# Indexer scores without POOL, and a convolution's running sum in PSUM

## The chip, the cores and the metric

One core of a Trainium2 chip runs the whole program. The metric is device time in microseconds (us), the median over runs of the same kernel. A profile is one further execution, recorded by the hardware profiler. The engines are PE (TensorE, matmuls), DVE (VectorE), ACT (ScalarE), POOL (GpSimd) and SP (SyncE, which here issues transfers). Matmuls write to PSUM, which is used here as eight banks of 128 partitions by 512 fp32 numbers; DVE and ACT read and write both PSUM and SBUF, and POOL is used here on SBUF alone.

## The reference

One decoder layer on 512 tokens of width 1024, batch 1, everything in fp32. After an RMSNorm, one projection is split between a gated DeltaNet group (4 heads) and a sparse attention group; both are joined, and a cross attention and a SwiGLU feed-forward follow. Two places matter here. The first is the input of the DeltaNet heads: 12 blocks of 128 channels (q, k and v for 4 heads), each put through a causal convolution with four taps per channel and then silu. The second is the score of the indexer, which decides the 128 keys that each query keeps:

```python
dq, dk, dv, dz, db, da, cq, ckv, kix, wix = jnp.split(h @ w_in[l], offs, axis=-1)
qkv = jax.nn.silu(causal_depthwise_conv(jnp.concatenate([dq, dk, dv], axis=-1), conv_w[l]))
...
rel = jax.nn.relu(jnp.einsum('bqhd,bsd->bqhs', qi, k_idx))       # 8 indexer heads
score = jnp.einsum('bqh,bqhs->bqs', wi, rel).astype(jnp.float32)
score = jnp.where(key_pos[None, None, :] <= tq[None, :, None], score, -jnp.inf)
_, idx = lax.top_k(score, k_sel)                                 # k_sel = 128
```

## The kernel before

Tokens run along the free dimension, channels along the partitions. fp32 matmuls are made from parts: every operand is split into a high and a low part, and `dense` (L149 to L151) issues three matmuls per 128 rows of the contraction, 24 for a projection of 128 channels. Weights come by DMA (`wraw`), ACT makes the high part `wh` (L141), and POOL or DVE subtracts it to give the low part `wl` (L142).

The order of the text is not the order on the chip. A scheduler reorders the instructions of each engine before the launch, within what data and buffers allow. The stages, as they are written: the input columns of the sparse group; transposes and norms (L328 to L331); the indexer's scores (L400 to L419, with the mask of future keys by POOL's `affine_select` in L421); four projections (k0, q0, k1, q1); gates and decays of the DeltaNet heads (L428 to L465, `Dm` and `row` among their names); top-k by 16 rounds of `max` (L489, eight values at a time) and `match_replace` (L490) for each of three query tiles, ended by L493; the other eight projections; `vt` (L540), a product for the attention; preparation of the triangular systems (L637 to L671); inverses of their diagonal blocks on DVE (L678 to L718), which go through DRAM (`x_d`) and come back as `X`; two further levels of the inverse on PE (L726 on), the recurrence, the attention, and the dense layers, from about 275 us to the end.

`project` (L352 to L381) makes one block of channels: dense into a PSUM bank `o`; L367 (DVE) multiplies by the row of norms into `cp`; L369 and L377 (ACT) make two taps from shifted copies, `a` and `b`; L378 and L379 (DVE) add the other two taps to them; L380 (POOL) adds `a` and `b`, and L381 (ACT) applies silu. For two of the v blocks (m 9 and 11) a third tap is ACT's (L373), added by POOL (L374), and DVE has only L375.

The scores: for each of 8 heads and each of 3 query tiles (256, 384 and 512 keys) two matmuls fill a bank `oo[s]`. For heads other than 2 and 6 DVE takes relu and the weight in one operation (L414), from PSUM into one of four buffers of `rlb`, and POOL adds it to the score (L416); the first head writes the score itself. For heads 2 and 6 ACT takes relu into `rlb` (L418), and DVE multiplies by the weight and adds (L419).

PSUM banks in this phase have the tags g (3 banks), lg (2), tp (2) and o (1). `ps(tag)` gives a bank: "pj", used by the first four projections, means tp; "mm", used by the other eight, means lg and tp in turn; "at", used by the scores and most else, goes through g, g, lg, g, o, lg.

Of the kernel before, what the change touches and what calls it, by code (L numbers as in the profile page):

```python
# [10 lines left out]
FT = mybir.dt.float32  # L11
FR = mybir.dt.float32r
AF = mybir.ActivationFunctionType
OP = mybir.AluOpType
AX = mybir.AxisListType

T = 512
# [64 lines left out]
def hybrid_block(ctx, tc, I, out):  # L82
    nc = tc.nc
    pe, act, dve, pool, sp = nc.tensor, nc.scalar, nc.vector, nc.gpsimd, nc.sync
# [19 lines left out]
    def pool_of(name, side=None):  # L104
        return tc.alloc_tile_pool(name=name, bufs=1, reuse_waits="tile", side=side) if side else \
            tc.alloc_tile_pool(name=name, bufs=1, reuse_waits="tile")
# [15 lines left out]
    def ps(tag="at"):  # L122
        n_ps[0] += 1
        if tag not in banks:
            turn[tag] = turn.get(tag, -1) + 1
            tag = alias[tag][turn[tag] % len(alias[tag])]
        return banks["pool"].tile([128, 512], FT, name=f"ps{n_ps[0]}", tag=tag, bufs=banks[tag])
# [40 lines left out]
    def weights(src, k0, kt, c0, cols, sub=None):  # L168
        return weights_split(*weights_raw(src, k0, kt, c0, cols), sub)

    def dense(h, l, XH, XL, n=T, o=None, order=None):
        o = ps("mm")[:, :n] if o is None else o
        order = order or range(len(XH))
        for k in order:
            mm3(o, h[:, k, :], l[:, k, :], XH[k], XL[k], k == order[0], k == order[-1])
        return o
# [42 lines left out]
    def par(name, k=0):  # L219
        return prT[:, PAR[name] + k:PAR[name] + k + 1]  # L220
# [75 lines left out]
    gp = pool_of("gp", "right")  # L296
# [1 line left out]

    wq = gp.tile([128, 2, 2, 512], FR, name="wq", tag="NT")
    wu = gp.tile([128, 2, 2, 512], FR, name="wu", tag="OGl")  # L300
    rlb = gp.tile([128, 4, 512], FT, name="rlb", tag="A")
    for w_, name in ((wq, "w_qidx"), (wu, "w_uq")):
        raw, _ = weights_raw(I[name][0], 0, 2, 0, 512)
        split(w_[:, 0], w_[:, 1], raw)
# [5 lines left out]
    for t in range(NT):  # L310
# [13 lines left out]
        for d in range(2):  # L324
            dve.tensor_scalar(kx[:, t * 128 + 64 * d:t * 128 + 64 * d + 64], kix_, st[:, 0:1], rs[:, 0:1],
                              op0=OP.subtract, op1=OP.mult)
        dve.scalar_tensor_tensor(ckv_, ckv_, rs[:, 2:3], gkv_b, op0=OP.mult, op1=OP.mult)
        for d in range(2):  # L328
# [4 lines left out]
                          None, op0=OP.mult)  # L333
# [18 lines left out]
    def project(kind, h, bank="mm", sub=pool):  # L352
        def c(shape=(128, T)):
            n_t[0] += 1
            return cvp.tile(list(shape), FT, name=f"cp{n_t[0]}", tag="cp", bufs=6)

        m = {"q": h, "k": 4 + h, "v": 8 + h}[kind]
        wh, wl = weights(w_in, 0, 8, m * 128, 128, sub)
        o = dense(wh, wl, XH, XL, o=ps(bank))
        if kind == "k" and QK[h] is None:  # L360
            QK[h] = gdn.tile([128, 2, T], FT, name=f"QK{h}", tag=f"QK{h}")
        if kind == "v":
            vtok[h] = gdn.tile([128, NT, 128], FT, name=f"vtok{h}", tag=f"vtok{h}")
        dst = vtok[h].rearrange("p c d -> p (c d)") if kind == "v" else QK[h][:, 0 if kind == "k" else 1, :]
        cp = c((128, T + 4))
        pool.memset(cp[:, 0:3], 0.0)
        dve.tensor_tensor(cp[:, 3:T + 3], o, Rrow, op=OP.mult)  # L367
        a, b = c(), c()
        act.activation(a, cp[:, 0:T], AF.Identity, scale=par("conv_w", m))  # L369
        if m in (9, 11):  # L370
            d_ = c()
            act.activation(b, cp[:, 1:T + 1], AF.Identity, scale=par("conv_w", 12 + m))
            act.activation(d_, cp[:, 2:T + 2], AF.Identity, scale=par("conv_w", 24 + m))  # L373
            pool.tensor_tensor(b, b, d_, op=OP.add)  # L374
            dve.scalar_tensor_tensor(a, cp[:, 3:T + 3], par("conv_w", 36 + m), a, op0=OP.mult, op1=OP.add)  # L375
        else:
            act.activation(b, cp[:, 1:T + 1], AF.Identity, scale=par("conv_w", 12 + m))  # L377
            dve.scalar_tensor_tensor(a, cp[:, 2:T + 2], par("conv_w", 24 + m), a, op0=OP.mult, op1=OP.add)  # L378
            dve.scalar_tensor_tensor(b, cp[:, 3:T + 3], par("conv_w", 36 + m), b, op0=OP.mult, op1=OP.add)  # L379
        pool.tensor_tensor(a, a, b, op=OP.add)  # L380
        act.activation(dst, a, AF.Silu)  # L381


    masks = dsa.tile([128, 1152], FT, name="masks")
# [1 line left out]
    score = {t: masks[:, SEG[t][0]:SEG[t][0] + SEG[t][1]] for t in SEG}  # L386
# [13 lines left out]
    for pr_ in range(4):  # L400
        st = qst[pr_]
        for t in (1, 2, 3):
            n = SEG[t][1]
            tt = slice(t * 128, (t + 1) * 128)
            oo = [ps()[:, :n] for _ in range(2)]
            for s in range(2):
                pe.matmul(oo[s], st[s][:, tt], kidl[:, :n], start=True, stop=False)
                pe.matmul(oo[s], st[s][:, tt], kidh[:, :n], start=False, stop=True)
            for s in range(2):
                hd = 2 * pr_ + s  # L410
                rl = rlb[:, (pr_ * 6 + t * 2 + s) % 4, :n]
                w_ = widx[:, 8 * t + hd:8 * t + hd + 1]
                if hd not in (2, 6):
                    dve.tensor_scalar(rl if hd else score[t], oo[s], 0.0, w_, op0=OP.max, op1=OP.mult)  # L414
                    if hd:
                        pool.tensor_tensor(score[t], score[t], rl, op=OP.add)  # L416
                    continue
                act.activation(rl, oo[s], AF.Relu)  # L418
                dve.scalar_tensor_tensor(score[t], rl, w_, score[t], op0=OP.mult, op1=OP.add)  # L419
    for t in (1, 2, 3):  # L420
        pool.affine_select(score[t][:, t * 128:], score[t][:, t * 128:], pattern=[[-1, 128]], compare_op=OP.is_ge,  # L421
                           fill=FUT, base=0, channel_multiplier=1)
# [1 line left out]
    for kind, h in (("k", 0), ("q", 0), ("k", 1), ("q", 1)):  # L424
        project(kind, h, bank="pj", sub=dve)
# [410 lines left out]
    for i, (kind, h) in enumerate([(k, h) for h in (2, 3) for k in "kq"] + [("v", h) for h in range(4)]):  # L836
        steps(gt, 1 if i % 2 else 2)
        project(kind, h)
# [6 lines left out]
    A = gp.tile([128, 4, NT, 128], FT, name="A", tag="A")  # L845
# [287 lines left out]
```

## Time and profile before

| what | us |
|---|---|
| median of 3 runs | 857.08 (856.7 to 859.29) |
| profiled execution | 855.63 |
| its span (first to last instruction) | 853.8 |
| PE busy in the span | 824.2 |

In the rows below, engines and operations are named as above; "x4" behind an operation means that the row groups four instructions, and a row of a timeline gives start, duration, and in brackets how long the engine was idle before it and what it waited for. Durations of neighbouring instructions of an engine can overlap a little.

### The profile page before, as it was taken

To read this page: it belongs to the slowest core of one execution; us is meant where nothing else is said; L and a number is where in the kernel's file an instruction comes from. 1 tells how busy PE (TensorE), PEld (TensorE's weight loads), DVE (VectorE), ACT (ScalarE), POOL (GpSimd) and SP (SyncE) were. 2 spreads that over 40 slices of the span, in tenths; PEclk is the share of its full clock that TensorE was granted. 3 is DMA by queue.
4 is the path that set the end of the run, shared out by engine and by line. 5 is a ranking of instruction groups with operands and counts; after the bars stand their busy time and mean duration, and the time that the engine had idled before them with its cause. 6 is when DMAs were issued, how large, how long until landed. Compare 5 with 4: busy or idle time off the path is not lost.

```text
span 853.8 us, 11022 instructions
## 1 busy us (share of the span) xinstructions
PE 824.2 (97%) x4122; PEld 679.5 (80%) x4122; DVE 489.6 (57%) x817; ACT 366.3 (43%) x721; POOL 211.4 (25%) x217
## 2 busy tenths in 40 slices
PE   9998999779998999999999999999999999999996
PEld 8876787578766889888877888888888888888885
DVE  7787999967555545464555445543355443245542
ACT  6675666417656544354444442221133331223332
POOL 5549577853211231000003221110011110001122
PEclk9999999889999999999999999999999999999999
DMA  8530322146525234343313533333323333332302
GB/s 288 149 102 26 125 74 72 35 95 165 131 57 198 68 93 137 99 137 107 96 55 106 166 99 99 91 92 111 91 83 99 99 98 99 99 90 83 99 25 98
DMA packets 134940, 88.30 MB, mean 103 GB/s; under 512 B 10304, under 2 KB 122344, under 8 KB 134888
## 3 DMA queue, kind: packets, MB, share of 16 engines
q1 hardware_dynamic: 131848, 85.87, 34.5%
q10 hardware_dynamic: 3040, 1.75, 0.7%
q8 instruction: 32, 0.52, 0.3%
q14 instruction: 20, 0.16, 0.1%
HBM read 76.84 MB, written 4.99 MB: 96 GB/s over the span
## 4 chain that ended last, share of the span: by engine, by line
PE 79%; DVE 12%; POOL 2%; ACT 2%; issue 2%; DMA 2%; SPq 0%; POOLq 0%; DVEq 0%; ACTq 0%
PE ps L149 21%; PE ps L150 21%; PE ps L151 21%; DVE masks L490 3%; DVE m L489 2%; DVE cp L378 1%; PE ps L607 1%; PE ps L1078 1%; PE ps L1077 1%; PE ps L1076 1%; PE ps L291 1%; PE ps L952 1%; PE ps L954 1%; PE ps L953 1%; POOL masks L416 1%
## 5 line engine op out<-in xcount | busy, mean ns | idle before, releaser
L141 ACT ACTIVATE wh<-wraw 128x1024 fp32r<-128x1024 f32 x120 | 127.7, 1065 | 314.7 <-PE ps L150 169.4
L151 PE MATMUL ps<-XH,wl 128*128 128x512 f32 x512 | 201.0, 393 | 0.0
L149 PE MATMUL ps<-XH,wh 128*128 128x512 f32 x512 | 200.6, 392 | 0.2 <-ACT wh L141 0.2
L150 PE MATMUL ps<-XL,wh 128*128 128x512 f32 x512 | 199.9, 390 | 0.0
L142 DVE TENSOR_TENSOR wl<-wraw,wh 128x1024 fp32r<-128x1024 f32 x108 | 154.3, 1430 | 67.9 <-ACT wh L141 67.6
L149 PEld LDWEIGHTS ps<-XH,wh 128*128 128x128 f32 x512 | 96.2, 188 | 20.7 <-issue 0.6
L151 PEld LDWEIGHTS ps<-XH,wl 128*128 128x128 f32 x512 | 96.1, 188 | 19.7 <-POOL wl L142 0.3
L150 PEld LDWEIGHTS ps<-XL,wh 128*128 128x128 f32 x512 | 96.2, 188 | 19.5
L1047 POOL TENSOR_TENSOR t2k<-t2k,t2k 128x512 f32<-128x512 f32 x22 | 29.4, 1336 | 291.0 <-DVE t2k L1046 283.9
L258 POOL TENSOR_TENSOR acc<-acc,t2k 128x512 f32<-128x512 f32 x21 | 37.4, 1779 | 182.2 <-ACT t2k L257 181.8
L1046 DVE TENSOR_TENSOR t2k<-ps,row 128x512 f32<-128x512 f32 x22 | 15.2, 691 | 67.9 <-PE ps L151 67.9
L151 PE MATMUL ps<-HH,wl 128*128 128x512 f32 x128 | 50.0, 393 | 0.0
L149 PE MATMUL ps<-HH,wh 128*128 128x512 f32 x128 | 49.9, 390 | 0.0
L150 PE MATMUL ps<-HL,wh 128*128 128x512 f32 x128 | 49.6, 390 | 0.0
L1058 DVE TENSOR_TENSOR XR<-ps,XR 128x512 f32<-128x512 f32 x16 | 11.1, 692 | 51.9 <-PE ps L151 51.9
L1044 DVE TENSOR_TENSOR t2k<-ps,row 128x512 f32<-128x512 f32 x22 | 15.2, 691 | 36.0 <-PE ps L151 36.0
L142 POOL TENSOR_TENSOR wl<-wraw,wh 128x1024 fp32r<-128x1024 f32 x12 | 29.5, 2464 | 18.4 <-ACT wh L141 18.4
L888 DVE TENSOR_TENSOR XR<-ps,XR 128x512 f32<-128x512 f32 x16 | 11.0, 691 | 34.0 <-PE ps L151 34.0
L489 DVE MAX8 m<-masks 128x8 f32<-128x512 f32 (+2 forms) x48 | 26.7, 556 | 4.4 <-POOL masks L421 3.6
L150 PEld LDWEIGHTS ps<-HL,wh 128*128 128x128 f32 x128 | 24.0, 188 | 5.1
L151 PEld LDWEIGHTS ps<-HH,wl 128*128 128x128 f32 x128 | 24.0, 188 | 4.9
L149 PEld LDWEIGHTS ps<-HH,wh 128*128 128x128 f32 x128 | 24.0, 188 | 4.9
(398 smaller groups left out, 1659.3 us busy)
## 6 DMA issues: line engine op xcount, KB each, us to landing
wraw<-in_w_gate SPq DMA_DIRECT2D x22, 512.0 KB, 3.6
wraw<-in_w_up SPq DMA_DIRECT2D x22, 512.0 KB, 3.7
wraw<-in_w_down SPq DMA_DIRECT2D x20, 512.0 KB, 3.8
wraw<-in_w_in SPq DMA_DIRECT2D x16, 512.0 KB, 3.7
wraw<-in_w_xkv SPq DMA_DIRECT2D x16, 512.0 KB, 3.8
wraw<-in_w_out SPq DMA_DIRECT2D x8, 512.0 KB, 4.0
wraw<-in_w_xq SPq DMA_DIRECT2D x8, 512.0 KB, 3.7
wraw<-in_w_xo SPq DMA_DIRECT2D x8, 512.0 KB, 3.8
```

Of the source, the lines that this page charges most:

```text
L141: act.activation(h, src, AF.Copy)
L142: (sub or dve).tensor_tensor(l, src, f32(h), op=OP.subtract)
L149: pe.matmul(o, lh, rh, start=start, stop=False)
L150: pe.matmul(o, lh, rl, start=False, stop=False)
L151: pe.matmul(o, ll, rh, start=False, stop=stop)
L258: pool.tensor_tensor(self.acc, self.acc, s_, op=OP.add)
L489: dve.max(m8, score[t])
L490: dve.match_replace(score[t], m8, score[t], MARK)
L1044: dve.tensor_tensor(s1, og_, Rrow2, op=OP.mult)
L1046: dve.tensor_tensor(s2, ou_, Rrow2, op=OP.mult)
L1047: pool.tensor_tensor(s1, s1, s2, op=OP.mult)
L1058: dve.tensor_tensor(XR[m], o, XR[m], op=OP.add)
```

## The change

Two edits. In the scores, the buffers `rlb` go; for heads 1 to 7 ACT takes relu in place, in the PSUM bank, and DVE multiplies that by the head's weight and adds it to the score. Head 0 stays as it was. POOL has no part in it any more. In `project`, the running sum `a` lies in a PSUM bank of the same kind as `o`: ACT writes the first tap there, DVE adds the second-last tap there, and the last tap is added by DVE into a new SBUF buffer `e_`, to which POOL adds `b`. For m 9 and 11, DVE reads `a` from PSUM too. Since both `o` and `a` now come from the tags "mm" or "pj", a projection takes two banks in turn instead of one. Lines of the new kernel are lower by 1 from L302 on and by 3 from L420 on.

```diff
-    rlb = gp.tile([128, 4, 512], FT, name="rlb", tag="A")
...
         dve.tensor_tensor(cp[:, 3:T + 3], o, Rrow, op=OP.mult)
-        a, b = c(), c()
+
+        a, b = ps(bank), c()
         act.activation(a, cp[:, 0:T], AF.Identity, scale=par("conv_w", m))
         if m in (9, 11):
             d_ = c()
             act.activation(b, cp[:, 1:T + 1], AF.Identity, scale=par("conv_w", 12 + m))
             act.activation(d_, cp[:, 2:T + 2], AF.Identity, scale=par("conv_w", 24 + m))
             pool.tensor_tensor(b, b, d_, op=OP.add)
-            dve.scalar_tensor_tensor(a, cp[:, 3:T + 3], par("conv_w", 36 + m), a, op0=OP.mult, op1=OP.add)
         else:
             act.activation(b, cp[:, 1:T + 1], AF.Identity, scale=par("conv_w", 12 + m))
             dve.scalar_tensor_tensor(a, cp[:, 2:T + 2], par("conv_w", 24 + m), a, op0=OP.mult, op1=OP.add)
-            dve.scalar_tensor_tensor(b, cp[:, 3:T + 3], par("conv_w", 36 + m), b, op0=OP.mult, op1=OP.add)
-        pool.tensor_tensor(a, a, b, op=OP.add)
-        act.activation(dst, a, AF.Silu)
+        e_ = c()
+        dve.scalar_tensor_tensor(e_, cp[:, 3:T + 3], par("conv_w", 36 + m), a, op0=OP.mult, op1=OP.add)
+        pool.tensor_tensor(e_, e_, b, op=OP.add)
+        act.activation(dst, e_, AF.Silu)
...
-                rl = rlb[:, (pr_ * 6 + t * 2 + s) % 4, :n]
                 w_ = widx[:, 8 * t + hd:8 * t + hd + 1]
-                if hd not in (2, 6):
-                    dve.tensor_scalar(rl if hd else score[t], oo[s], 0.0, w_, op0=OP.max, op1=OP.mult)
-                    if hd:
-                        pool.tensor_tensor(score[t], score[t], rl, op=OP.add)
+                if hd == 0:
+                    dve.tensor_scalar(score[t], oo[s], 0.0, w_, op0=OP.max, op1=OP.mult)
                     continue
-                act.activation(rl, oo[s], AF.Relu)
-                dve.scalar_tensor_tensor(score[t], rl, w_, score[t], op0=OP.mult, op1=OP.add)
+                act.activation(oo[s], oo[s], AF.Relu)
+                dve.scalar_tensor_tensor(score[t], oo[s], w_, score[t], op0=OP.mult, op1=OP.add)
```

The scheduler also moves instructions. Three places follow, each as the rows of one engine in their order.

PE, the end of the first projection (`ps_655`) and the start of the second (`ps_697`) before, and the rows between the two after; the lines L328 to L331 are transposes of the input `U`:

```order
L151 MATMUL ps_655<-XH_91,wl_652 128x512
L331 MATMUL ps_347<-cst,U_148 128x128 [waits DVE_49,PE_49]
L149 MATMUL ps_697<-XH_84,wh_693 128x512 [waits Activation_49]
L150 MATMUL ps_697<-XL_92,wh_693 128x512
L151 MATMUL ps_697<-XH_84,wl_694 128x512
```

```order
L328 MATMUL ps_343<-cst,U_148 128x128 [waits Activation_49]
L328 MATMUL ps_344<-cst,U_148 128x128 [waits PE_49]
L329 MATMUL ps_345<-cst,t2k_347 128x128 [waits PE_49]
L328 MATMUL ps_343<-cst,U_149 128x128 [waits Activation_49]
L328 MATMUL ps_344<-cst,U_149 128x128
L328 MATMUL ps_343<-cst,U_150 128x128 [waits Activation_49]
L328 MATMUL ps_344<-cst,U_150 128x128
L329 MATMUL ps_345<-cst,t2k_347 128x128 [waits DVE_49]
L330 MATMUL ps_346<-cst,U_149 128x128 [waits DVE_49]
L329 MATMUL ps_345<-cst,t2k_347 128x128 [waits DVE_49]
L330 MATMUL ps_346<-cst,U_150 128x128 [waits DVE_49]
L149 MATMUL ps_697<-XH_84,wh_693 128x512 [waits DVE_49]
```

The second projection waits for DVE now, where it waited for ACT, and eleven transposes stand ahead of it.

DVE, the start of the scores, before and after (`masks` holds the scores, `sm_349` and `sm_348` the heads' weights, `prT` the taps, `cp_` and `ps_811` the convolution's buffers):

```order
L414 TENSOR_SCALAR masks<-ps_523,sm_349 128x256 [waits PE_49]
L414 TENSOR_SCALAR masks<-ps_532,sm_349 128x384 [waits PE_49]
L414 TENSOR_SCALAR rlb<-ps_524,sm_349 128x256 [waits PE_49]
L378 SCALAR_TENSOR_TENSOR cp_809<-cp_806,prT,cp_809 128x512 [waits Activation_49,Pool_49]
L414 TENSOR_SCALAR rlb<-ps_533,sm_349 128x384 [waits PE_49]
L414 TENSOR_SCALAR masks<-ps_541,sm_349 128x512 [waits PE_49]
L379 SCALAR_TENSOR_TENSOR cp_810<-cp_806,prT,cp_810 128x512 [waits Activation_49]
L414 TENSOR_SCALAR rlb<-ps_542,sm_349 128x512 [waits PE_49,Pool_49]
```

```order
L413 TENSOR_SCALAR masks<-ps_522,sm_348 128x256 [waits PE_49]
L413 TENSOR_SCALAR masks<-ps_531,sm_348 128x384 [waits PE_49]
L377 SCALAR_TENSOR_TENSOR ps_811<-cp_808,prT,ps_811 128x512 [waits Activation_49,Pool_49]
L413 TENSOR_SCALAR masks<-ps_540,sm_348 128x512 [waits PE_49]
L379 SCALAR_TENSOR_TENSOR cp_816<-cp_808,prT,ps_811 128x512 [waits DVE_49]
L416 SCALAR_TENSOR_TENSOR masks<-ps_523,sm_348,masks 128x256 [waits Activation_49]
L416 SCALAR_TENSOR_TENSOR masks<-ps_532,sm_348,masks 128x384 [waits Activation_49]
L416 SCALAR_TENSOR_TENSOR masks<-ps_541,sm_348,masks 128x512 [waits DVE_49,Activation_49]
```

The waits for POOL at the reuse of `rlb` are gone, and every multiply-add waits for ACT's relu.

DVE, the last rounds of top-k and the end of the diagonal blocks, before and after (L710 before and L707 after is the copy that is sent to DRAM):

```order
L489 MAX m_991<-masks 128x8 [waits DVE_49]
L710 COPY cv_1786<-cv_1762 128x256 [waits DVE_49]
L490 MATCH_REPLACE masks<-m_991,masks 128x512 [waits DVE_49]
L489 MAX m_991<-masks 128x8 [waits DVE_49]
L493 TENSOR_SCALAR masks<-masks 128x512
L490 MATCH_REPLACE masks<-m_991,masks 128x384 [waits DVE_49]
L489 MAX m_991<-masks 128x8 [waits DVE_49]
L493 TENSOR_SCALAR masks<-masks 128x384
L490 MATCH_REPLACE masks<-m_991,masks 128x256 [waits DVE_49]
L493 TENSOR_SCALAR masks<-masks 128x256 [waits DVE_49]
```

```order
L700 TENSOR_TENSOR cv_1776<-cv_1771,cv_1773 128x512 [waits DVE_49]
L702 TENSOR_REDUCE cv_1777<-cv_1776 128x64 [waits DVE_49]
L703 TENSOR_TENSOR cv_1776<-cv_1773,cv_1777 128x512 [waits DVE_49]
L705 TENSOR_REDUCE cv_1773<-cv_1776 128x8x8 [waits DVE_49]
L707 COPY cv_1797<-cv_1773 128x256 [waits DVE_49]
L725 TENSOR_TENSOR cv_1822<-ps_1817,cst 128x512 [waits PE_49]
```

Before, the last of the top-k instructions stood behind the copy; now the copy is the last of this stretch.

## Rows read from the trace of the kernel before

**Rows 1.** The page's first part: busy time, share of the span, instructions.

```profile
PE 824.2 (97%) x4122; PEld 679.5 (80%) x4122; DVE 489.6 (57%) x817; ACT 366.3 (43%) x721; POOL 211.4 (25%) x217
```

**Rows 2.** Busy time by stretch: stretch, length, engines (instructions), PE clock, DMA share, GB/s.

```profile
61.40:85.90 24.50, 22.25 (x104) 15.02 (x104) 19.19 (x32) 14.80 (x36) 22.42 (x22) 1.00 0.12 32
85.90:106.30 20.40, 19.28 (x88) 15.20 (x87) 19.48 (x54) 12.79 (x48) 11.10 (x16) 1.00 0.39 130
106.30:176.10 69.80, 64.47 (x285) 51.17 (x285) 68.85 (x151) 38.15 (x100) 50.71 (x44) 0.95 0.21 55
183.30:275.00 91.70, 84.44 (x658) 68.70 (x658) 56.67 (x157) 55.51 (x178) 27.57 (x41) 0.98 0.52 140
275.00:853.80 578.80, 571.13 (x2700) 476.95 (x2699) 272.35 (x326) 200.90 (x294) 67.89 (x54) 1.00 0.33 97
```

**Rows 3.** Timeline of DVE, 36 to 180 us: start, duration, what it does.

```profile
36.67 0.68 DVE L367 TENSOR_TENSOR cp<-ps,row 128x512 f32<-128x512 f32 x1
...
61.41 1.00 DVE L414 TENSOR_SCALAR masks<-ps,sm 128x256 f32<-128x256 f32 x2
...
85.89 0.69 DVE L489 MAX8 m<-masks 128x8 f32<-128x512 f32 x1 [3.58 <-POOL masks L421]
...
106.31 0.69 DVE L367 TENSOR_TENSOR cp<-ps,row 128x512 f32<-128x512 f32 x1 [0.24 <-PE ps L151]
...
116.44 2.92 DVE L378 SCALAR_TENSOR_TENSOR cp<-cp,prT,cp 128x512 f32<-128x512 f32 x1
...
175.73 0.39 DVE L710 COPY cv<-cv 128x256 f32<-128x256 f32 x1
...
179.38 0.29 DVE L493 TENSOR_SCALAR masks<-masks 128x256 f32<-128x256 f32 x1
```

**Rows 4.** Timeline of PE, 33 to 184 us.

```profile
33.82 0.48 PE L149 MATMUL ps<-XH,wh 128*128 128x512 f32 x1
...
100.44 0.58 PE L149 MATMUL ps<-XH,wh 128*128 128x512 f32 x1
...
106.12 0.39 PE L149 MATMUL ps<-XH,wh 128*128 128x512 f32 x1
...
183.28 5.99 PE L726 MATMUL ps<-X,NTt 128*128 128x128 f32 x32 [4.40 <-DMA X<-x_d]
```

**Rows 5.** POOL by shape, 61.4 to 86: instructions, busy us, mean ns, idle before.

```profile
L416 POOL TENSOR_TENSOR masks<-masks,rlb 128x512 f32<-128x512 f32 x5 | 6.6, 1314 | 0.0
L421 POOL TENSOR_SCALAR_AFFINE_SELECT masks<-masks 128x128 f32<-128x128 f32 x3 | 0.8, 287 | 0.1
```

**Rows 6.** DVE by shape, 61.4 to 85.9 us.

```profile
L414 DVE TENSOR_SCALAR rlb<-ps,sm 128x512 f32<-128x512 f32 x5 | 3.7, 745 | 1.1 <-POOL masks L416 1.0
L414 DVE TENSOR_SCALAR rlb<-ps,sm 128x384 f32<-128x384 f32 x5 | 3.0, 609 | 0.5 <-POOL masks L416 0.5
L414 DVE TENSOR_SCALAR rlb<-ps,sm 128x256 f32<-128x256 f32 x5 | 2.4, 478 | 0.1
L419 DVE SCALAR_TENSOR_TENSOR masks<-rlb,sm,masks 128x512 f32<-128x512 f32 x2 | 1.5, 739 | 0.0
```

**Rows 7.** Timeline of ACT, 77 to 100 us.

```profile
77.35 0.98 ACT L418 ACTIVATE rlb<-ps 128x512 f32<-128x512 f32 x2 [0.28 <-DVE masks L419]
...
87.94 1.22 ACT L141 ACTIVATE wh<-wraw 128x1024 fp32r<-128x1024 f32 x1
...
98.26 1.10 ACT L540 ACTIVATE vt<-ps 128x512 f32<-128x512 f32 x2
```

**Rows 8.** DVE by shape, 106.3 to 176.1 us.

```profile
L378 DVE SCALAR_TENSOR_TENSOR cp<-cp,prT,cp 128x512 f32<-128x512 f32 x6 | 10.5, 1752 | 0.0
L379 DVE SCALAR_TENSOR_TENSOR cp<-cp,prT,cp 128x512 f32<-128x512 f32 x6 | 4.8, 796 | 0.0
L375 DVE SCALAR_TENSOR_TENSOR cp<-cp,prT,cp 128x512 f32<-128x512 f32 x2 | 3.7, 1863 | 0.0
```

**Rows 9.** Timeline of POOL, at 116 us.

```profile
116.40 2.40 POOL L142 TENSOR_TENSOR wl<-wraw,wh 128x1024 fp32r<-128x1024 f32 x1
```

## The prediction

> **What bounds the kernel now.** I read the page's first part, then the busy times by stretch, then the timelines of the four engines at the places where the change acts. TensorE is busy for 824.2 us, 97% of the span [rows 1], so only what shortens its gaps or its slow stretches can move the end. The stretches show where those are [rows 2]: from 275 us on, PE is busy for 571.13 of 578.8 us with dense matmuls, and nothing in the change touches that. The change acts between 61 and 176 us, and there PE's busy time is no proof that PE is the bound: it has filler, projections that the scheduler pushes into any gap. What cannot be filled is a chain over DVE. DVE is busy for 68.85 of 69.80 us between 106.3 and 176.1, 19.48 of 20.40 between 85.9 and 106.3, and 19.19 of 24.50 in the score stage [rows 2]. At 175.73 it ends the inverse of the diagonal blocks (L710); those go through DRAM and PE needs them at 183.28, after a gap of 4.40 us that ends with that transfer (X) [rows 3, 4]. So I follow DVE's three stretches up to X, and take what lies behind X as moved along with it.
>
> **Score stage, 61.41 to 85.89 (24.5 us).** DVE begins it without a wait, and its first top-k instruction begins at 85.89 after 3.58 us of waiting for POOL's affine_select, which stands behind POOL's chain of additions [rows 3]. That chain is the bound here: 15 additions, five of each width, in series on each score tile; the five widest take 6.6 us [rows 5]. The change takes all of them away. In their place DVE has 24 instructions that read PSUM. A PSUM read with one operation costs 0.478, 0.609 and 0.745 us for 256, 384 and 512 columns, and DVE's multiply-add from SBUF costs 0.739 for 512 [rows 6], so I price the new multiply-add from PSUM like the old PSUM read: 8 x (0.478 + 0.609 + 0.745) = 14.7 us. With the two convolution instructions that stand among them (2 x 0.74), one affine_select of 0.29 [rows 5] and 0.3 of handing over, that is 16.8 us: **-7.7 us**, first top-k instruction at 78.2. ACT's 21 relus stay below this: two of 512 columns take 0.98 us [rows 7], so 21 take at most 10.3. Neither relu in place nor a DVE write into PSUM has a row; from the nearest ones, 0.49 on ACT and 0.74 on DVE, I take no extra cost. Bounds -9 (no gaps between instructions, which overlap a little) to -4 (each of the 24 multiply-adds waits 0.15 us for its relu).
>
> The Trainium skill, VectorE: DVE Perf Modes, section "The TRN2 errata", speaks against this price: it gives a DVE instruction a fixed 58 cycles from SBUF and 120 from PSUM. That would be an estimated 62 cycles, some 0.065 us, for each multiply-add that moves to PSUM; 28 of them (6 in the score stage, 22 in the convolutions) make some 1.8 us. The rows decide otherwise: 512 columns take 0.745 from PSUM and 0.739 from SBUF [rows 6].
>
> **From the first top-k instruction to the next convolution (L367 at 106.31).** This was 20.4 us. DVE alone would now be through at 78.2 + 19.5 (its busy time [rows 2]) = 97.7. But ACT has a chain of its own in this stretch: from its last relu, which ended at 78.33, through the gate decays to the copies of vt, which end at 99.36 [rows 7], 21.0 us. The relus now end with DVE's score stage, near 77.2, not a full 7.7 us earlier. One weight split of 1.22 in the chain (L141 [rows 7]) moves behind, with the projection that it feeds; ACT is busy for only 12.79 of the 20.40 us [rows 2], so some of the rest is waiting for PE, and I take 0.7 off: 77.2 + 21.0 - 1.2 - 0.7 = 96.3. Behind it PE needs a projection, 100.44 to 106.12 [rows 4], 5.7 us, before L367 has anything to read: 102.0 instead of 106.3. Of the 7.7 us, **+3.4 go back** (bounds +1 to +6): this is where I expect the largest loss.
>
> **The convolutions, 106.3 to 176.1.** Their multiply-adds with two SBUF inputs are stretched there: L378 takes 1.752 on average for 6, L379 0.796 for 6, L375 1.863 for 2 [rows 8], where the same form undisturbed takes 0.739 [rows 6]. The L378 of 2.92 us at 116.44 begins beside POOL's 2.40 us subtraction at 116.40 and ends just behind it [rows 3, 9]; L367, which reads one operand from PSUM, takes 0.69 [rows 3]. After the change, L378, L379 and L375 have one SBUF operand and one in PSUM. If the stretch goes: 6 x (1.752 - 0.74) + 6 x (0.796 - 0.74) + 2 x (1.863 - 0.74) = 6.1 + 0.3 + 2.2 = 8.6, **-8.7 us** with rounding (bounds -3 if the stretch passes to the DVE instructions that still have two SBUF operands, -8.7).
>
> The Trainium skill, SBUF - State Buffer, section "Who interferes with whom", has a rule for that: a DVE instruction with two SBUF inputs shuts out a GpSimd instruction that reads SBUF, and the reverse, for the whole instruction; with one SBUF input it does not. The trace agrees (2.92 beside 2.40 us). By the rule the whole 8.7 go; without it, only the chance meetings of the new order do.
>
> **What moves in front of X.** The order of DVE changes at the end of this stretch: before, L710 stood ahead of the last top-k instructions, which end at 179.67; after, all of top-k stands ahead of it. Those 179.67 - 176.12 = 3.55 us [rows 3] now lie on the chain. Some instructions of the prepare stage also slide behind L367 and there are handovers from PE, estimated at three to four instructions of 0.69: 2.3. Together **+5.9** (bounds +4 to +7).
>
> **At no cost.** The second projection's matmuls (33.82 [rows 4]) now wait until L367, which began at 36.67 [rows 3], has released the only bank left to `o`: 3.5 us of PE, filled partly with eleven transposes that the scheduler puts there. DVE's queue began the score stage at 61.41 without a wait, so I take 0 (bounds -1 to +2.5). POOL's and ACT's count per convolution is unchanged: 0. Behind X, 91.7 us with PE busy for 84.44 and 578.8 us of dense work [rows 2] move along: 0 (bounds -1 to +4).
>
> **Sum.** -7.7 + 3.4 - 8.7 + 5.9 = -7.1. PE's own work in the third stretch, 64.47 busy of 69.80 plus the projection pushed behind (5.7), gives 70.2 behind 102.0 = 172.2, against DVE's L710 at about 169 and X some 7.2 us later (176.12 to 183.28), 176; PE is not last. Against the profiled execution, 855.63, that is 848.5; this execution is 1.45 us below the median of the runs, 857.08, so I predict **850.0** as a median.
>
> **Rivals.**
> 1. *DVE sets the second stretch too.* If ACT's chain shrinks further, because its pieces wait for DVE and not the reverse, L367 comes at 98 instead of 102: 4 us more, 846 or a little less. For it: DVE's 19.48 of 20.40; against it: ACT's copies at 99.36 and the projection behind them. 13%.
> 2. *The score gain is eaten whole.* If ACT needs its 21.0 us and PE its projections as before, L367 stays near 106 and only the convolutions count: -8.7 + 5.9 = -2.8, about 854 (852 to 854.5). 14%.
> 3. *Nothing arrives.* The stretch of L378 passes to other instructions with two SBUF operands (-3 instead of -8.7), and half of the score gain is lost: near 857 (854.5 to 859.7). 12%.
> 4. *Slower by a loop over PSUM banks.* `o` and `a` take banks of the same two tags in turn, so `o` always comes from the one and `a` from the other. A projection can then start only when L367 of an earlier one has read its `o`. Where `o` has one bank, PE stops at each handover for 0.24 (PE to DVE) + 0.69 (L367) [rows 3] = 0.93; if all 11 following projections stop, +10.2 us, against -7.1: 860. It decides if PE waits at more than eight of them. For it: in the first four `o` has just one bank. Against it: the later eight have two, and PE has filler there. 9%.
>
> The forecast itself, 846.5 to 852, has 52%.
>
> **How the numbers follow.** 0.3%, about 2.6 us, is what a measurement of this kernel can tell from no change. Faster than 854.5: forecast 52%, rival 1 13%, rival 2 14%: 0.79. Within: 0.12. Slower: 0.09. The range, 843 to 857, takes in the forecast with its bounds (-7.1 with -9 for the scores and +1 for the giving back is -10.8, and some more behind X: 843), rivals 1 and 2 and half of rival 3.
>
> **What would show it.** Right: POOL's additions are gone and the first top-k instruction begins near 78; the next L367 near 102, behind ACT's chain; L378 at 0.74; X's matmuls near 176 instead of 183.28; a span some 7 us shorter, the same from 275 on. Wrong: multiply-adds from PSUM above 0.85, or DVE waiting for ACT in the score stage; PE idle on DVE at each projection's start; X early, but PE not earlier at the dense stages.

## The result, and the profile after

The changed kernel takes 843.99 us (median of 4 runs, 842.92 to 844.85), against 857.58 us for the kernel before beside it: a ratio of 0.9838, 95% interval 0.982 to 0.9856. A second set of runs gave 843.95 us and 0.9835 (0.9817 to 0.9852). The forecast was 850.0 with a range of 843 to 857; the direction holds, the range holds by 1 us at its lower edge, and the size is almost twice the 7.1 us of the sum. The profiled execution took 844.85 us, 10.8 less than that of before, 855.63, which turned out to lie at the lower edge of what that kernel does (855.3 to 860.73 in later runs). The trace places those 10.8; the other 3 us of the 13.6 between the medians are the spread of executions.

The busy times by stretch of the changed kernel, cut at the same events as [rows 2] (start of the scores, first top-k instruction, next convolution, copy that ends the diagonal blocks, X, dense layers), with the same columns:

```profile
61.90:77.20 15.30, 15.30 (x77) 11.49 (x76) 14.37 (x31) 14.80 (x33) 4.57 (x6) 1.00 0.13 36
77.20:97.90 20.70, 19.19 (x94) 14.42 (x93) 18.81 (x52) 17.80 (x66) 9.91 (x15) 1.00 0.26 90
97.90:169.40 71.50, 68.98 (x319) 56.97 (x318) 67.13 (x164) 39.32 (x101) 51.29 (x46) 0.98 0.24 65
169.40:177.40 8.00, 2.42 (x11) 1.68 (x9) 0.00 (x0) 3.69 (x6) 4.02 (x5) 0.93 0.52 91
177.40:264.20 86.80, 82.95 (x658) 69.95 (x660) 55.36 (x156) 54.22 (x175) 25.58 (x38) 0.95 0.52 138
264.20:843.10 578.90, 570.84 (x2700) 476.86 (x2700) 274.37 (x326) 201.38 (x295) 66.99 (x54) 1.00 0.33 99
```

The score stage fell from 24.5 to 15.3 us; the next stretch kept its 20.4 (20.7); the convolutions' stretch grew, from 69.8 to 71.5, though the second half of the gain was to come from there; and the stretch behind X, which the prediction moved along unchanged, fell from 91.7 to 86.8. From the dense layers on nothing changed (578.80 and 578.90).

DVE's timeline of the changed kernel at the events of [rows 3]:

```profile
61.91 1.00 DVE L413 TENSOR_SCALAR masks<-ps,sm 128x256 f32<-128x256 f32 x2
...
77.22 0.69 DVE L486 MAX8 m<-masks 128x8 f32<-128x512 f32 x1
...
97.90 0.67 DVE L366 TENSOR_TENSOR cp<-ps,row 128x512 f32<-128x512 f32 x1
...
163.47 0.28 DVE L490 TENSOR_SCALAR masks<-masks 128x256 f32<-128x256 f32 x1
...
168.99 0.39 DVE L707 COPY cv<-cv 128x256 f32<-128x256 f32 x1
```

PE's, at the events of [rows 4]:

```profile
91.78 0.79 PE L149 MATMUL ps<-XH,wh 128*128 128x512 f32 x1
...
177.44 6.51 PE L723 MATMUL ps<-X,NTt 128*128 128x128 f32 x32 [5.62 <-DMA B<-tb_d]
```

The copy ends at 169.38, where the forecast had it (about 169), 6.74 us earlier than before; X starts 5.84 us earlier. (X's last transfer landed at 177.06; the releaser that the row names is a later transfer of the same queue. Before, the row named X.) The other 4.9 us are gained behind X.

The price of the new operations, DVE by shape in the score stage, to set beside [rows 6]:

```profile
L416 DVE SCALAR_TENSOR_TENSOR masks<-ps,sm,masks 128x512 f32<-128x512 f32 x7 | 5.2, 742 | 0.0
L416 DVE SCALAR_TENSOR_TENSOR masks<-ps,sm,masks 128x384 f32<-128x384 f32 x7 | 4.3, 607 | 0.0
L416 DVE SCALAR_TENSOR_TENSOR masks<-ps,sm,masks 128x256 f32<-128x256 f32 x7 | 3.3, 475 | 0.0
L377 DVE SCALAR_TENSOR_TENSOR ps<-cp,prT,ps 128x512 f32<-128x512 f32 x1 | 0.8, 754 | 0.0
```

A multiply-add from PSUM costs what one from SBUF does (742 and 739 ns), one that writes into PSUM 754; and none waited for its relu.

In the convolutions' stretch (97.9 to 169.4 us), DVE by shape, to set beside [rows 8]:

```profile
L379 DVE SCALAR_TENSOR_TENSOR cp<-cp,prT,ps 128x512 f32<-128x512 f32 x8 | 5.9, 736 | 0.2 <-ACT ps L369 0.2
...
L377 DVE SCALAR_TENSOR_TENSOR ps<-cp,prT,ps 128x512 f32<-128x512 f32 x6 | 4.4, 741 | 0.1
...
L662 DVE TENSOR_TENSOR A<-ps,Dm 128x256 f32<-128x256 f32 x6 | 2.5, 415 | 0.0
...
L695 DVE TENSOR_TENSOR cv<-cv,cv 128x12 f32<-128x12 f32 x2 | 2.5, 1242 | 0.0
...
L692 DVE TENSOR_TENSOR cv<-cv,cv 128x16 f32<-128x16 f32 x1 | 1.9, 1875 | 0.0
L688 DVE TENSOR_SCALAR cv<-cv 128x256 f32<-128x256 f32 x1 | 1.2, 1237 | 1.5 <-DMA cv<-n_d 1.5
```

The multiply-adds take 10.3 us instead of 19.0: the 8.7 us are there to the tenth. But one L692 and one L695, tiny products of the diagonal blocks that take 0.15 to 0.16 us elsewhere in this trace, now took 1.88 and 2.33 us (the mean of 1242 ns mixes 2.33 and 0.16), and L688 1.24 instead of 0.53. Before, products of these blocks were stretched too, but others: L706, which is L703 now (before, then after):

```profile
L706 DVE TENSOR_TENSOR cv<-cv,cv 128x64 f32<-128x64 f32 x2 | 3.9, 2010 | 0.0
```

```profile
L703 DVE TENSOR_TENSOR cv<-cv,cv 128x64 f32<-128x64 f32 x2 | 0.5, 270 | 0.0
```

The two L706 lost 3.5 us before; L688, L692 and L695 lose 4.6 now. So some 1.1 us more is lost on the blocks than before.

Behind X, what PE waits for, before and after (columns: who waited for whom: us in all, times, longest):

```profile
PE ps L825 <- DVE cv L821: 3.3, 2, 2.9
PE ps L582 <- DVE c L592: 1.4, 3, 0.9
PE ps L598 <- ACT PT L600: 1.4, 3, 0.7
PE ps L598 <- ACT sm L594: 0.4, 1, 0.4
```

```profile
PE ps L595 <- ACT PT L597: 1.5, 1, 1.5
PE ps L595 <- ACT sm L591: 1.4, 2, 1.0
...
PE ps L822 <- DVE cv L818: 0.3, 1, 0.3
...
PE ps L579 <- DVE c L589: 0.2, 1, 0.2
```

L825 before is L822 after: the transposes of the recurrence's last output, the last step ahead of the dense layers. Before, the scheduler had put the recurrence's last products (L810) between the attention's last (L607), so that the norm and gate behind them ran on DVE and ACT while PE had nothing left. In the changed kernel they stand well ahead, and that wait fell from 3.3 to 0.3 us, 3.0 of the 4.9.

### The profile page after: what moved, and what is told of

The parts are those of the page before. It is cut to its first block, busy times and chain, and to the rows that moved or that the text cites. A ratio compares the mean times of both kernels' runs of the same rounds, so it can differ in the third digit from the quotient of the medians.

```text
span 843.1 us, 11038 instructions
## 1 busy us (share of the span) xinstructions
PE 817.6 (97%) x4122; PEld 680.3 (81%) x4122; DVE 477.3 (57%) x817; ACT 371.6 (44%) x736; POOL 191.3 (23%) x202
## 4 chain that ended last, share of the span: by engine, by line
PE 87%; DVE 4%; ACT 4%; DMA 2%; issue 1%; POOL 0%; SPq 0%; POOLq 0%; DVEq 0%; ACTq 0%
PE ps L149 23%; PE ps L151 23%; PE ps L150 23%; PE ps L604 1%; PE ps L723 1%; PE ps L778 1%; PE ps L1075 1%; PE ps L1074 1%; PE ps L1073 1%; PE ps L595 1%; PE ps L951 1%; PE ps L949 1%; PE ps L950 1%; PE ps L731 1%; PE ps L634 1%
## 5 line engine op out<-in xcount | busy, mean ns | idle before, releaser
L1055 DVE TENSOR_TENSOR XR<-ps,XR 128x512 f32<-128x512 f32 x16 | 11.1, 692 | 51.9 <-PE ps L151 51.9
L142 POOL TENSOR_TENSOR wl<-wraw,wh 128x1024 fp32r<-128x1024 f32 x12 | 29.0, 2420 | 15.3 <-ACT wh L141 15.3
```

The costliest lines, as they stand in the source:

```text
L142: (sub or dve).tensor_tensor(l, src, f32(h), op=OP.subtract)
L1055: dve.tensor_tensor(XR[m], o, XR[m], op=OP.add)
```

## The experiments

Events of each profiled execution, in us (the start of PE's dense layers is the first matmul of `odh`):

| kernel | first top-k | copy ends | X | dense | X to dense | span |
|---|---|---|---|---|---|---|
| before | 85.89 | 176.12 | 183.28 | 275.55 | 92.3 | 853.8 |
| changed | 77.22 | 169.38 | 177.44 | 264.49 | 87.1 | 843.1 |
| scores_only | 78.76 | 174.04 | 181.45 | 267.16 | 85.7 | 845.5 |
| conv_only | 84.67 | 178.21 | 186.28 | 270.30 | 84.0 | 848.5 |
| before_tail | 86.72 | 176.90 | 184.06 | 275.17 | 91.1 | 853.5 |
| relu_sbuf | 76.83 | 171.01 | 179.23 | 262.58 | 83.4 | 840.8 |
| after_topk_late | 76.27 | 163.99 | 172.11 | 261.70 | 89.6 | 841.4 |
| after_topk_late_tail | 77.42 | 165.22 | 173.49 | 261.12 | 87.6 | 839.4 |
| relu_late_tail | 78.00 | 164.41 | 170.92 | 260.54 | 89.6 | 838.8 |
| relu_late_tail_neg | 77.95 | 166.03 | 172.50 | 261.84 | 89.3 | 840.1 |
| scores_dvesplit | 78.24 | 176.38 | 183.33 | 269.65 | 86.3 | 847.9 |
| after_again | 77.63 | 169.89 | 177.97 | 265.58 | 87.6 | 844.3 |

### The two edits apart

scores_only has the change's lines in the scores and the old `project`; conv_only the reverse. The core of each:

```diff
-                    dve.tensor_scalar(rl if hd else score[t], oo[s], 0.0, w_, op0=OP.max, op1=OP.mult)
-                        pool.tensor_tensor(score[t], score[t], rl, op=OP.add)
+                act.activation(oo[s], oo[s], AF.Relu)
+                dve.scalar_tensor_tensor(score[t], oo[s], w_, score[t], op0=OP.mult, op1=OP.add)
```

```diff
-        a, b = c(), c()
+        a, b = ps(bank), c()
...
+        dve.scalar_tensor_tensor(e_, cp[:, 3:T + 3], par("conv_w", 36 + m), a, op0=OP.mult, op1=OP.add)
```

> The edit to the scores alone; the convolutions keep their running sum in SBUF. Theory A (the gain has three sources: score stage, convolutions, and the order at the end of recurrence and attention, which the scheduler has changed here too): top-k starts near 77 and the next convolution near 98, as in the changed kernel (77.22 and 97.90); L378 still averages 1.5 us or more; from X's matmuls to the dense layers about 87 us instead of 91.7. In all 857.6 - 9 (scores) - 4.9 (end) = about 844 to 847. Theory B (the scores are worth only what the convolutions, then the bound, let through): the stretch of the convolutions grows by what the scores give, and the time stays within 2 us of 852.

Measured: 846.77 us, ratio 0.9878 (0.9857 to 0.9899), 11.1 below before. Theory A in the total, and in the stage: top-k at 78.76. But X comes only 1.8 us earlier; 6.6 us are gained behind it.

> The edit to the convolutions alone; the scores go through POOL as before. Theory A: the multiply-adds fall from 1.75 to 0.74 us with POOL's work unchanged, but PE and the moved instructions give most of those 8.7 us back; the next convolution stays near 106; the end of recurrence and attention has the new order (-4 to -5): 850 to 853. Theory B (the stretched multiply-adds were worth their whole 8.7 us): 8.7 + 4.9 below before, 844.

Measured: 856.0 us, ratio 0.9969 (0.9946 to 0.9992), 1.9 below before; by the median both theories missed. But its twelve runs lie in two groups: four at 850.55 to 851.52 with a mean granted clock of 0.986 to 0.988, inside theory A's range and some 7 below before, and eight at 855.14 to 859.01 with 0.977 to 0.983. The profiled execution is the lowest of the first group; no profile shows where the second lost its clock. In the profiled one the multiply-adds did fall, to 0.74 us, and X came 3.0 us later than before: the way from the first top-k instruction to the copy grew from 90.2 to 93.5 us, with all of top-k ahead of the copy. PE had used up its filler and stood still for X:

```profile
186.28 5.47 PE L727 MATMUL ps<-X,NTt 128*128 128x128 f32 x32 [16.05 <-DMA X<-x_d]
```

The two savings, 11.1 and 1.9, add up to 13.0, near the 13.6 of both. That is no proof that they add: with the first group of conv_only alone the sum would be near 18.

### Why the multiply-adds were stretched

In scores_only they still are (1536 ns for 6). This kernel is scores_only with one more change: the last eight projections' subtractions run on DVE.

```diff
-        project(kind, h)
+        project(kind, h, sub=dve)
```

> The edit to the scores alone, and for the last eight projections DVE instead of POOL subtracts the weights' high part (L142). The multiply-adds keep two SBUF operands. Theory A (they are stretched because POOL's 2.4 us subtractions run beside them): L377, 1.54 us on average in the kernel with the score edit alone, falls to 0.75 to 0.95, with only POOL's additions of 1.3 us left to meet. Rival (two SBUF operands are slow of themselves, or the stretch is due to PE's or ACT's traffic): 1.4 us or more. The time tells little, as DVE has eight subtractions of some 1.4 us more to do.

One run: 849.65 us. L377 by shape, in scores_only and then here:

```profile
L377 DVE SCALAR_TENSOR_TENSOR cp<-cp,prT,cp 128x512 f32<-128x512 f32 x6 | 9.2, 1536 | 0.1
```

```profile
L377 DVE SCALAR_TENSOR_TENSOR cp<-cp,prT,cp 128x512 f32<-128x512 f32 x6 | 5.1, 846 | 0.0
```

With the 2.4 us subtractions off POOL and both operands still in SBUF, the mean is 0.846: five of the six take 0.73 to 0.74, and the sixth takes 1.40, beginning beside one of POOL's additions of 1.29 us. So the stretch was POOL's. conv_only shows the other half: POOL keeps its subtractions of 2.4 us, one operand lies in PSUM, and the multiply-adds take 0.73 to 0.76. That is the rule of the Trainium skill, SBUF - State Buffer, "Who interferes with whom", from both sides.

### Relu into SBUF

The changed kernel with `rlb` back and all 21 relus put there:

```diff
-                act.activation(oo[s], oo[s], AF.Relu)
-                dve.scalar_tensor_tensor(score[t], oo[s], w_, score[t], op0=OP.mult, op1=OP.add)
+                rl = rlb[:, (pr_ * 6 + t * 2 + s) % 4, :n]
+                act.activation(rl, oo[s], AF.Relu)
+                dve.scalar_tensor_tensor(score[t], rl, w_, score[t], op0=OP.mult, op1=OP.add)
```

> The changed kernel, but ACT's relu goes to four SBUF buffers, as it did for heads 2 and 6 before, and DVE's multiply-add reads two SBUF operands. Theory A (what the scores gain is POOL's chain of additions gone, not where the relu lies): score stage within 1.5 us of 15.3, in all 843.5 to 846. Rival (PSUM in place is what pays, since two SBUF operands are stretched beside POOL): multiply-adds at 1.0 us and more for 512 columns, stage 18 us or more, in all 847 or more.

Measured: 842.67 us (842.61 to 842.89), ratio 0.9825 (0.9804 to 0.9847), 0.8 below theory A's range; its condition holds, the score stage took 15.9 us (60.92 to 76.83), and the rival's 847 is far off. The multiply-adds read two SBUF operands:

```profile
L418 DVE SCALAR_TENSOR_TENSOR masks<-rlb,sm,masks 128x384 f32<-128x384 f32 x7 | 5.3, 752 | 0.0
L418 DVE SCALAR_TENSOR_TENSOR masks<-rlb,sm,masks 128x512 f32<-128x512 f32 x7 | 5.2, 738 | 0.0
L418 DVE SCALAR_TENSOR_TENSOR masks<-rlb,sm,masks 128x256 f32<-128x256 f32 x7 | 3.3, 473 | 0.0
```

Only what meets the little that POOL still does there is stretched: one of the seven with 384 columns took 1.64 us beside POOL's addition of 1.37, which lifts the mean from 607 to 752. What the scores gain is POOL's chain of additions gone; where the relu lies is of little account. All eight runs of the changed kernel (842.92 to 846.03) lie above these four, by 1.3 us in the median; but the two never ran beside each other, and the intervals of their ratios overlap (0.9825, and 0.9838 and 0.9835), so that a gain by relu in SBUF is not shown. The copy and X come later in it, and the stretch behind X is shorter.

### The order at the end, alone

The kernel before; PE's last eight products of the attention are forced behind the recurrence's last four. Up to there every engine keeps the order of before; behind it the preparation of the cross attention moves too.

```diff
+                late[0] = pe.matmul(O[:, h * 128:(h + 1) * 128], A[:, h, c, :], V[:, h, :], ...)
...
+            with tc.issue_after(late[0].ins) if pr_ == 3 else nullcontext():
                 for kb in range(NT):
```

> The kernel before, whole; only PE's order at one place is forced: the last four products of the recurrence go ahead of the last eight products of the attention, as the scheduler has it in the changed kernel. Up to there every engine's order is that of before. Theory A (the 4.9 us that the changed kernel gains behind X come from that order): PE's wait of 2.88 us at the end goes, 852.5 to 855. Rival (they come from X being early, or from something else in that stretch): within 1 us of before.

Measured: 853.46 us, ratio 0.995 (0.993 to 0.997): 4.4 below before. The wait at the end is halved, from 3.3:

```profile
PE ps L828 <- DVE cv L824: 1.7, 2, 1.3
```

So the order at the end, which neither edit touches, with what moves behind it, is worth 0.3 to 0.7% by the interval in this kernel, and part of what the change gained behind X can be put down to it.

### Is DVE's way to X still what counts?

```diff
-    for g_ in (gates(), gt):
-        for _ in g_:
-            pass
+    for _ in gates():
+        pass
+    steps(gt, 2)
...
-    diagonal_blocks()
+    last_copy = diagonal_blocks()
+    with tc.issue_after(last_copy.ins):
+        for _ in gt:
+            pass
```

> The changed kernel, with the last two rounds of top-k and its closing instructions forced behind the copy that ends the diagonal blocks, as they stood in part before. This takes some 8 us of DVE's work off the way to X; the scheduler then gives the end of recurrence and attention the order of before. Theory A (what moved in front of X, and the order at the end, are terms of one sum): the copy ends near 162 to 165 instead of 169.4, X's matmuls start 3 to 6 us earlier, and the end is 2 to 4 us longer again: 841 to 845. Rival (PE's filler, not DVE, sets X's start now): X's matmuls stay near 177 and the time rises by the end's 2 to 4 us to 846 to 848.

Measured: 843.43 us, ratio 0.9833 (0.9815 to 0.9852), beside 843.95 for the unchanged one:

> The changed kernel, unchanged, beside the others on one chip: 843 to 845 by its earlier runs. With relu into SBUF 842.61 to 842.89 was measured; if that is faster, every run here lies above 842.89.

Theory A, event by event: the copy at 163.99, X 5.3 us earlier, and the scheduler gave back the old order at the end, with its wait. One thing more changed: PE waits 0.90 us for X here, and its granted clock in the 10 us behind X is 1.00; in the changed kernel it waits 5.62 us, and the clock there is 0.72 (0.50, the lower level of 1.2 GHz, in the first 4.6 us). 84 matmuls fall into these 10 us, there 65. The wait at the end:

```profile
PE ps L823 <- DVE cv L819: 3.4, 2, 2.9
```

Then the same with that order forced as above:

> The kernel with the last two rounds of top-k behind the copy (843.43 us), and the order at the end forced as in the forced kernel before; up to there nothing moves. Theory A (that order alone costs what it cost before): PE's wait of 2.9 us for DVE at the end goes, 839.5 to 841.5. Rival (the end is bound by DVE or ACT whichever way PE is ordered): 842.5 to 844.

Measured: 841.35 us, ratio 0.9803 (0.9784 to 0.9821), the wait 1.7. Theory A's 839.5 to 841.5 holds. The runs of the two don't overlap (842.64 to 845.32, 840.89 to 841.79), and the kernel before took the same beside both (858.79 and 858.95): the order is worth 2.1 us here.

### All together, and one instruction more

Relu into SBUF, top-k behind the copy and the forced order at the end, by the three diffs above.

> Relu into SBUF, the last two rounds of top-k behind the copy, and the order at the end forced (last products of the recurrence ahead of the attention's last eight). If the three are terms of one sum: 842.7 - 3 to 5 for X, with the end's cost half avoided: 838 to 842. Rival (PE's work, the same in all these kernels, is the bound up to the dense layers, and an earlier X only moves its waiting): 842 to 844.

Measured: 840.67 us (840.62 to 842.03), ratio 0.9802 (0.9786 to 0.9817): the lowest median of all, 3.3 below the changed kernel beside it. PE waits only 1.94 us for X there. Its diagonal blocks begin with an instruction of 3.73 us with one SBUF operand, the change of sign; taking it off DVE should bring the copy forward:

```diff
-        dve.tensor_scalar(blk, blk, -1.0, None, op0=OP.mult)
+        act.activation(blk, blk, AF.Copy, scale=-1.0)
```

> The kernel of 840.67 us with one instruction moved: the change of sign at the start of the diagonal blocks (L691, one SBUF operand, on DVE 3.73 us beside POOL's subtraction and memset) is done by ACT; the order of PE is the same and that of DVE but for it. Theory A (this stretch too lies on the way to X): the copy 2 to 3 us earlier, at about 161.5, and since PE waits 1.94 us for X, 838.7 to 840. Rival (the copy is bound by the round trip through DRAM and ACT's queue): 840.5 or more.

Measured: 841.76 us (840.04 to 841.87), ratio 0.9801 (0.9777 to 0.9824): no gain, as the rival has it, but for a reason that I had not named. The next product now waited for POOL's memset of a tile that it reads; it began at 155.48 instead of 153.86, and the copy ended 1.6 us later:

```profile
155.48 2.32 DVE L695 TENSOR_TENSOR cv<-cv,cv 128x12 f32<-128x12 f32 x1 [3.93 <-POOL cv L684]
```

## Why the prediction was right where it was right, and where it failed

- **Score stage (-7.7): right, a little small.** From its start to the first top-k instruction 15.3 us instead of 16.8 and of 24.5, -9.2; it began 0.5 later. POOL's chain was the bound, the new instructions cost what the old ones did, and DVE never waited for a relu. What the sum did not see is that ACT has as little room left there as DVE: it is busy for 14.80 of the 15.30 us. The table that gives an instruction with a PSUM source more fixed cycles (the Trainium skill, VectorE: DVE Perf Modes, "The TRN2 errata") is borne out by no row of the multiply-adds: 742 from PSUM, 739 and 738 ns from SBUF.
- **3.4 us given back before the next convolution: failed.** That stretch took 20.68 us instead of 20.42; 0.3 us went back. The step said that PE's projection starts behind ACT's chain. It does not depend on it: it began at 91.78, while that chain's last copies of vt (L537) were still to come. Rival 1 had the right place, with 98 for the next L367; it is at 97.90.
- **Convolutions (-8.7): right in the instructions, wrong as a gain.** 19.0 became 10.3 us, as summed. But from the next convolution to the copy DVE needs 71.5 us instead of 69.8, where I had 67.0. The step that failed is the +5.9 for what moves in front of X. It came out at +10.4: 3.55 of top-k, as summed, but in place of the 2.3 for moved instructions and handovers two pairs of L662 more (1.7), 3.4 of idle time (4.4 against 0.95 by the windows; the rows name PE, the round trip of the blocks through DRAM, and ACT), and about 1.1 by which L688, L692 and L695 were stretched beyond what L706 lost; some 0.6 are not assigned. So the largest part that it lacked is DVE's waiting. The stretch that passes to others, for which I had named a bound of -3, took only about 1.1 of the 8.7. conv_only's profile points the same way: with the multiply-adds at 0.74, X came 3.0 us later.
- **Their sum at X: right by errors that cancel.** Copy at 169.38 against about 169; X -5.84 against -7.1, with 0.9 more from copy to X than before.
- **Behind X, 0: failed, and this is why the size was off.** 4.9 us (in the profiled executions) came from a stretch that I took as moved along. 3.0 of them are the wait at its end, which goes with the order of PE's last products; before_tail shows that forcing this order, with what moves behind it, is worth 4.4 us by the medians (0.3 to 0.7%) in before, though it only halves the wait. I read the moved top-k rounds as a pure loss of 3.55 us in front of X. They were one side of a trade: in after_topk_late, where they stand behind again, X gains 5.3 us, the old order returns at the end, and the time is the same within 0.1%. I compared the order at two places on DVE and one on PE, none of them behind X.
- **Rivals 2 to 4 did not happen.** No loop over PSUM banks: in the convolutions' stretch PE lists no wait for the instructions that read `o`; the first projections cost at most the 0.5 us by which the scores began later.
- **What stays open:** why X to dense takes 83.4 to 92.3 us in kernels with the same work. In the two pairs of profiled executions that differ in the order at the end alone, it is worth 1.2 us (before, whose profiled execution is a short one) and 2.0 us (after_topk_late); no run here isolates the rest. There is a pattern: where DVE ended top-k some 13 us or more ahead of X, the stretch takes 83.4 to 87.6 us; where it ended 3.6 us ahead of X or behind it, 87.6 to 92.3. That fits the trade, but the order at the end and the clock differ between these kernels too, so that it is not shown as a cause.

## What to carry to other kernels

Price a change not only where it acts: under a scheduler that reorders, compare the order of every engine up to the point where the program is surely the same again, above all at the end of a stage whose results the next one needs as a whole. An instruction made shorter on a chain that another engine stretches pays only as far as the stretch doesn't pass to the next instruction with two SBUF operands and the chain doesn't meet another wait: look at what else runs beside POOL, and at what the chain will wait for once it is shorter. And if additions on POOL are the series that sets a stage, giving them to DVE as a multiply-add cost DVE nothing where it read that PSUM bank anyway (742 against 745 ns for 512 columns); the price was ACT's, which took over the relus.

## What the runs showed of the hardware that was not expected

An instruction with a single SBUF operand can be held by POOL too. In relu_sbuf the change of sign on DVE, 0.53 us in the kernel before, took 3.61 us, and ended with POOL's memset:

```profile
147.54 3.61 DVE L690 TENSOR_SCALAR cv<-cv 128x256 f32<-128x256 f32 x1 [0.34 <-issue]
```

```profile
146.61 2.40 POOL L142 TENSOR_TENSOR wl<-wraw,wh 128x1024 fp32r<-128x1024 f32 x1
148.94 0.32 POOL L682 MEMSET cv<- 128x256 f32 x1
149.19 1.82 POOL L850 MEMSET Y<- 128x2048 f32 x1
```

The Trainium skill, SBUF - State Buffer, "Who interferes with whom", names `tensor_scalar` among the instructions that can run in a mode that takes the ports shared with GpSimd; the trace agrees, and it shows the wait going over three POOL instructions in a row. So the prediction had put that rule too widely, as if one SBUF input were always safe. In relu_late_tail a `tensor_scalar` of 16 columns (L768) took 1.64 us, where its like took 0.16 in the kernel before (L765), and ended with a subtraction of POOL's. And ACT's relu into PSUM is no dearer than into SBUF for 512 columns: 596 ns against 598 in the kernel before and 629 in relu_sbuf.
